# A two-layer encoder trunk: gates and branch projections with tokens as the stationary operand, seven task lanes, another order of the projections, one transform in plain fp32

## The chip, the cores and the metric

The kernel runs on one core of one Trainium2 chip, as one program. The metric is device time in microseconds (us). Before the change it is 1631.18 us, the median of three runs (1630.85 to 1631.53).

## The reference, cut to what matters

The trunk has two layers over 256 tokens of width 1024, all in float32. Each layer adds three sub-layers to x. The first one is where the change lies:

```python
h = rmsnorm(x, mix_norm_g)
proj = h @ w_in          # q, k, v, z, xbc, dt, f_in, gate_logit: 14400 columns
y_attn    = attention(q, k, v) @ w_b_attn      #  512 -> 1024, three groups merged
y_ssd     = ssd(xbc, dt, z)    @ w_b_ssd       # 2048 -> 1024
f = fft2(f_in (256 tokens, 6 groups, 256), axes=(tokens, channels), "ortho").real
y_fourier = f @ w_b_fourier                    # 1536 -> 1024
gates = sigmoid(gate_logit + gate_bias)        # (256, 3, 1024)
merged = gates[0] * y_attn + gates[1] * y_ssd + gates[2] * y_fourier
x = x + merged @ w_out
```

Then come cross-attention into 256 memory tokens and a SwiGLU feed-forward part of width 2816; the change does not touch these two.

## The kernel before, in words

**Split products.** Weights reach the chip as fp32. Each piece of weights (usually 128 x 2048 numbers, 1 MB) is split: ScalarE casts it to fp32r (`wh`, line 323), VectorE subtracts to get the rest (`wl`, line 324). Activations are kept as such a pair too. One product is then three fp32r matmuls on TensorE: high by high, high by low, low by high (`mm3`). Elsewhere (attention scores, the SSD products of lines 848 and 849, attention times values in line 648) a product is one plain fp32 matmul.

**Two forms of projection.** `lin` (lines 353 to 355) holds 128 tokens by 128 inputs as the stationary operand and streams 512 weight columns past it: the result has tokens on the partitions. `lina` (lines 414 to 416) holds 128 x 128 weights stationary and streams the 256 tokens: the result has output channels on the partitions. Before the change, the gate logits, the three branch projections and the x/B/C channels go through `lina`; q, k, v, z, the Fourier inputs, the output projection and cross-attention go through `lin`; the feed-forward part uses both.

**Pieces in order.** `stream_plan` writes out the order of the pieces from the list `ORDER`, and SyncE's DMA queue loads them in it. There are three buffers for raw pieces (`wr`) and three for split ones (`wh`, `wl`), so a split can start only when TensorE is done with the piece three before.

**Background tasks.** All that follows a projection (convolution, SSD, attention, Fourier, gating) is written as Python generators in queues called lanes ("n", "s", "a", "f"). Behind each piece, `pump` gives the lanes some us of credit, and `step` runs the next task's next stage, if the pools of 4 KB and 2 KB slots have room. A stage that says LATER waits for some pumps. When a slot is wanted and few are free, stages are run at once, whatever the credit. The tile framework then orders the instructions of each engine.

**Around the change.** `gates` (line 1013) applies tanh on ScalarE with the bias as a per-partition operand (line 1021). `branch` (line 1027) multiplies gate and projection into `mg` on VectorE (lines 1036 to 1039). `merge_fin` (line 1129) splits the merged channels as they are, since the output projection wants channels on the partitions. The Fourier inputs' even and odd token sums are split (lines 1088 to 1092), and `fourier_chunk` transforms positions with `mm3` on 128 x 128 tiles, in its first loop; the channel transform is a second `mm3`.

Of the kernel before, what the change touches and what calls it, by code (L numbers as in the profile page):

```python
# [34 lines left out]
LANES = ("n", "s", "a", "f")  # L35
# [10 lines left out]
ORDER = ("f0 f1 f2 bc k0 x0 G2 BF x1 q0 v0 q2 x2 q1 k1 v1 k2 v2 z1 x3 G0 z0 z2 z3 BA G1").split()  # L46


def stream_plan():
    plan = []  # L50

    def half(w, n0, h, k0=0):
        plan.append((w, k0 + 4 * h, 4, n0, 512))

    def full(w, n0):
        half(w, n0, 0)
        half(w, n0, 1)
# [9 lines left out]
    def blocks(w, kt, n):  # L67
        for n0 in range(0, 1024, n):
            plan.append((w, 0, kt, n0, n))

    for tok in ORDER:
        k, g = tok[0], int(tok[1]) if len(tok) > 1 and tok[1].isdigit() else 0
        if k == "f":
            full("w_in", F0 + 512 * g)
        elif k == "G":
            for c in range(4):
                wide("w_in", G0 + 1024 * g + 256 * c)
        elif tok == "BF":
            blocks("w_branch_fourier", 12, 128)
        elif tok == "BA":  # L80
            blocks("w_branch_attn", 4, 512)
# [24 lines left out]
    plan.append(("w_ffn_down", 20, 2, 0, 1024))  # L106
    return plan
# [5 lines left out]
POFF = [sum(PSIZE[:i]) for i in range(NPIECE + 1)]  # L113


def pack_weights(inputs):
    out = np.empty((L, POFF[-1]), np.float32)
# [54 lines left out]
def trunk(ctx: ExitStack, tc: tile.TileContext, a, out):  # L172
# [367 lines left out]
    def attn_group(l, g, qt, kt_, vt, gqk, R):  # L540
# [43 lines left out]
        O = R["O"]  # L584
        for tt in range(2):
# [23 lines left out]
            if tt or not g:  # L609
                free(bts[tt])  # L610
# [42 lines left out]
            else:  # L653
                for hh in range(4):
                    hs = slice(hh * P, hh * P + P)
                    o = O[:, tt, hs]
                    V.tensor_scalar(o, o, sc[:, 3, hh:hh + 1], None, op0=ALU.mult)
                    V.scalar_tensor_tensor(o, po[:, hs], sc[:, 0, hh:hh + 1], o, op0=ALU.mult, op1=ALU.add)
            yield 1.6
        free(qt, vt, kT)  # L660
        if g == 2:
            yield LATER
            yield 2, 0
            oT = R["oT"] = ftiles(1)
            for tt in range(2):
                pt = tp()
                for hh in range(4):
                    T.transpose(pt[:, hh * P:(hh + 1) * P], O[:, tt, hh * P:(hh + 1) * P], idn)
                put_f(pt, oT[0], tt, par=True)
                yield 0.7  # L670
            free(O)
            R["a"] = True
# [219 lines left out]
    def dft_parts(R):  # L892
        yield 3, 0
        r = s4([P, 6, P])
        nc.sync.dma_start(r, a["c_dft"])
        hi, lo = R["dft"] = s4([P, 6, P], F32R), s4([P, 6, P], F32R)
        A.copy(hi, r)
        V.tensor_sub(lo, r, hi.bitcast(F32))
        free(r)
        yield 0.9  # L900

    def fourier_chunk(l, c, f, FT, R):
# [5 lines left out]
        dh, dl = R["dft"]  # L908
# [23 lines left out]
        for cp_ in range(2):  # L932

            qc, qs = (t[:, :4 * n].rearrange("p (j k) -> p j k", j=4) for t, n in ((tp(), 66), (tp(), 64)))
            with ordered():
                for m, o, k0, k1 in ((2, qc, 0, 66), (4, qs, 64, 128)):
                    m += cp_
                    mm3(o, dh[:, m, :], dl[:, m, :], gp[0][:, cp_, :, k0:k1], gp[1][:, cp_, :, k0:k1], True, True)
# [50 lines left out]
    for l in range(L):  # L989
# [19 lines left out]
        gbc = sm([P, 24], "gbc", bufs=1)  # L1009
        nc.sync.dma_start(gbc, a["gateb"][l])  # L1010
        V.tensor_scalar(gbc, gbc, 0.5, None, op0=ALU.mult)
# [15 lines left out]
        def branch(act, np_, ga, fin=None):  # L1027
            first = not mg
            if first:
                mg.extend(s4([P, 4, S]) for _ in range(2))  # L1030

            def f(n0, ps):
                c, n = n0 // P, ps.shape[1]
                g_, m_ = (t[c // 4][:, c % 4:c % 4 + n, :] for t in (ga, mg))
# [5 lines left out]
                if fin:  # L1040
                    fin(c, n, m_)
            lina(act, np_, f)
# [24 lines left out]
        def xbc_pieces(blk, fin_of):  # L1067
            def f(n0, ps):
                pair = (n0 - X0) // 256 - blk // 2
                bg(conv_pair(ps, blk + 2 * pair, cw, fin_of(pair)))  # L1070
            lina(hb, 2, f)

        ys, FT, yT = {}, {}, {}
        bg(dft_parts(R), "f")
        for n, tok in enumerate(ORDER):
            k, g = tok[0], int(tok[1]) if tok[1].isdigit() else 0
            sg = [2] if n == 0 else None
            if k == "f":
                ft = (s4([P, 2, 512], F32R), s4([P, 2, 512], F32R))

                fs = []

                def f_done(tt, ch, ps, ft=ft, fs=fs):
                    if tt == 0:
                        fs.extend((s2([P, 512]), s2([P, 512])))
                        A.copy(fs[0], ps)
                        return
                    V.tensor_add(fs[1], fs[0], ps)
                    V.tensor_sub(fs[0], fs[0], ps)
# [7 lines left out]
            elif tok == "bc":  # L1097
# [4 lines left out]
                bg(cb_task(l, Bt, Ct, R))  # L1102
            elif k == "x":
                xT = s4([P, 2, 512])
                xbc_pieces(4 * g, lambda pr: x_fin([xT], pr))
                bg(ssd_group(l, g, xT, R, Dbc, ys))
# [4 lines left out]
            elif k == "z":  # L1111
                zt = s4([P, 2, 512])
                lin(hb, 2, lambda tt, ch, ps, zt=zt: A.activation(zt[:, tt, :], ps, AF.Silu))
                bg(ssd_gate(l, g, zt, ys, yT))
            elif k == "G":
                ga = gates(g)
            elif tok == "BF":
                drain_until(lambda: R.get("f") == 3, "f")
                branch(fl(FT), 8, ga)
                free(*FT.values(), ga)  # L1120
            elif tok == "BA":
                drain_until(lambda: "oT" in R and R.get("a"), "a")
                branch(fl(R["oT"]), 2, ga)
# [10 lines left out]
        branch(fl(yT), 8, ga, merge_fin)  # L1134
        free(*yT.values(), ga, mg)
# [21 lines left out]
        lin(fl(mT), 4, residual(gbx, hx), seg=[1, 3])  # L1157
# [271 lines left out]
```

## Time and profile before

| what | value |
|---|---|
| profiled execution, whole | 1631.55 us |
| its span | 1629.8 us |
| median of three runs | 1631.18 us |
| TensorE busy | 1611.2 us, 99% |
| VectorE busy | 1164.7 us, 71% |
| ScalarE busy | 974.2 us, 60% |
| 16 DMA engines, mean share of the weight queue | 54.0% |

How to read the rows further down. A row of a group of instructions gives line, engine, operation, output<-inputs by name, size of the stationary operand, shape of what streams through, count, then busy us in total and mean ns of one. A matmul's own duration includes the time in which the next one already runs, so what a stream of matmuls costs is read from the distance of their starts in the timeline. A timeline row is: start in us, duration in us, engine, line, operation, count; a chain row is: start, us until the next step, what. A row of waits is: who waited, for whom, us in total, times, longest. A row of windows is: stretch, its length, busy us of each engine with its count, the granted clock as a share of full speed, the DMA share, GB/s.

### The profile page before, as it was taken

Reading aid. Unit: us, or ns where it says so; the run is one execution under the profiler, and the core shown is the slowest. Engines: PE = TensorE matmul, PEld = TensorE weight load, DVE = VectorE, ACT = ScalarE, POOL = GpSimd, SP = SyncE. Lnnn points to the kernel's source line nnn. Section 1 sums busy time; section 2 is a strip of 40 time slices with the busy share of each in tenths; the row PEclk is TensorE's granted clock in tenths of the full one; section 3 lists DMA queues with packets and bytes.
Section 4 is the critical chain, followed back from the end, with each engine's and each line's share of the span. In section 5 each row is a group of like instructions: output and inputs, shape, how many; then the busy total and the mean of one; then the engine's idle time right before and its main releaser. Section 6 shows DMA issues by size and latency. Waiting matters only on the chain.

```text
span 1629.8 us, 25584 instructions
## 1 busy us (share of the span) xinstructions
PE 1611.2 (99%) x10354; PEld 1454.3 (89%) x10354; DVE 1164.7 (71%) x1803; ACT 974.2 (60%) x1639; POOL 45.9 (3%) x47
## 2 busy tenths in 40 slices
PE   7999999999999999999999999999999999999998
PEld 6899988898998888999879998888989988889997
DVE  6898878788966665555479988868888676665543
ACT  6566667778745665444355667677786357554441
POOL 0000000000100100000000000000000001000000
PEclk9999999999999999999999999999999999999999
DMA  8445754656556544555553567555455555445552
GB/s 280 152 153 188 237 202 149 203 172 178 194 177 228 178 156 156 206 181 192 181 170 123 175 213 226 195 170 180 168 187 194 182 206 181 143 158 179 183 189 93
DMA packets 84302, 296.52 MB, mean 182 GB/s; under 512 B 7529, under 2 KB 46825, under 8 KB 53976
## 3 DMA queue, kind: packets, MB, share of 16 engines
q1 hardware_dynamic: 84184, 294.89, 54.0%
q8 instruction: 81, 1.33, 0.3%
q14 instruction: 37, 0.30, 0.1%
HBM read 293.65 MB, written 1.22 MB: 181 GB/s over the span
## 4 chain that ended last, share of the span: by engine, by line
PE 94%; ACT 3%; DVE 2%; issue 1%; POOL 0%; DMA 0%; SPq 0%; DVEq 0%; ACTq 0%; POOLq 0%
PE acc L354 14%; PE acc L355 14%; PE acc L353 14%; PE acc L415 13%; PE acc L414 13%; PE acc L416 13%; PE tp L848 2%; ACT wh L323 2%; PE tp L353 1%; PE tp L355 1%; PE tp L354 1%; PE tp L849 1%; PE tp L473 1%; PE tp L648 1%; PE tp L603 1%; DVE wl L324 1%
## 5 line engine op out<-in xcount | busy, mean ns | idle before, releaser
L324 DVE TENSOR_TENSOR wl<-wr,wh 128x2048 fp32r<-128x2048 f32 (+2 forms) x260 | 573.3, 2207 | 283.9 <-ACT wh L323 283.3
L323 ACT CAST wh<-wr 128x2048 fp32r<-128x2048 f32 (+2 forms) x260 | 477.4, 1839 | 402.2 <-issue 181.2
L414 PE MATMUL acc<-s,wh 128*128 128x256 f32 x1856 | 527.9, 285 | 0.0
L415 PE MATMUL acc<-s,wh 128*128 128x256 f32 x1856 | 526.6, 284 | 0.0
L416 PE MATMUL acc<-s,wl 128*128 128x256 f32 x1856 | 525.5, 283 | 0.0
L353 PE MATMUL acc<-wh,s 128*128 128x512 f32 x1072 | 427.7, 399 | 0.0
L354 PE MATMUL acc<-wl,s 128*128 128x512 f32 x1072 | 424.4, 396 | 0.4 <-DVE wl L324 0.4
L355 PE MATMUL acc<-wh,s 128*128 128x512 f32 x1072 | 423.7, 396 | 0.0
L415 PEld LDWEIGHTS acc<-s,wh 128*128 128x128 f32 x1856 | 356.1, 192 | 1.3 <-issue 0.5
L414 PEld LDWEIGHTS acc<-s,wh 128*128 128x128 f32 x1856 | 355.8, 192 | 1.6 <-issue 0.9
L416 PEld LDWEIGHTS acc<-s,wl 128*128 128x128 f32 x1856 | 355.8, 192 | 0.0
L355 PEld LDWEIGHTS acc<-wh,s 128*128 128x128 f32 x1072 | 203.6, 190 | 41.6 <-issue 1.4
L353 PEld LDWEIGHTS acc<-wh,s 128*128 128x128 f32 x1072 | 203.9, 190 | 41.2 <-issue 1.9
L354 PEld LDWEIGHTS acc<-wl,s 128*128 128x128 f32 x1072 | 203.8, 190 | 41.0 <-issue 0.9
L689 DVE SCALAR_TENSOR_TENSOR s<-s,cw,s 128x253 f32<-128x253 f32 (+2 forms) x288 | 121.7, 476 | 1.1 <-ACT s L686 0.7
L820 ACT ACTIVATE s<-s,nacs 128x128 f32<-128x128 f32 x128 | 44.6, 394 | 15.2 <-DMA s<-dd 13.9
L823 ACT ACTIVATE s<-s,dt 128x128 f32<-128x128 f32 x128 | 43.8, 395 | 2.7 <-DVE s L604 2.1
L821 DVE SCALAR_TENSOR_TENSOR s<-s,nacs,s 128x128 f32<-128x128 f32 x128 | 41.5, 344 | 5.0 <-ACT s L820 5.0
L353 PE MATMUL tp<-s,s 128*128 128x256 f32 (+2 forms) x152 | 42.8, 284 | 1.7 <-ACT s L923 1.5
L355 PE MATMUL tp<-s,s 128*128 128x256 f32 (+2 forms) x152 | 42.6, 283 | 0.5 <-DVE s L1092 0.5
L354 PE MATMUL tp<-s,s 128*128 128x256 f32 (+2 forms) x152 | 42.4, 280 | 0.0
L489 DVE TENSOR_TENSOR s<-tp,s 128x512 fp32r<-128x512 f32 x56 | 36.6, 683 | 5.6 <-ACT s L488 5.6
(223 smaller groups left out, 1419.7 us busy)
## 6 DMA issues: line engine op xcount, KB each, us to landing
wr<-in_wstream SPq DMA_DIRECT2D x236, 1024.0 KB, 4.9
s<-dd SPq DMA_DIRECT2D x32, 512.0 KB, 5.3
wr<-in_wstream SPq DMA_DIRECT2D x16, 768.0 KB, 4.4
s<-vd SPq DMA_DIRECT2D x12, 256.0 KB, 6.1
wr<-in_wstream SPq DMA_DIRECT2D x8, 256.0 KB, 4.7
s<-in_ssd_norm_g SPq DMA_DIRECT2D x8, 256.0 KB, 5.4
s<-in_memT SPq DMA_DIRECT2D x4, 512.0 KB, 5.9
X<-in_x SPq DMA_DIRECT2D x2, 512.0 KB, 3.8
```

Source lines behind the costliest of these rows:

```text
L323: A.copy(hi[:, c], raw[:, c])
L324: V.tensor_sub(lo[:, c], raw[:, c], hi[:, c].bitcast(F32))
L353: T.matmul(o, sh, mh, start=start, stop=False)
L354: T.matmul(o, sh, ml, start=False, stop=False)
L355: T.matmul(o, sl, mh, start=False, stop=stop)
L414: T.matmul(o, hi[:, w0:w0 + P], sh[:, k, :], start=kt == 0, stop=False)
L415: T.matmul(o, hi[:, w0:w0 + P], sl[:, k, :], start=False, stop=False)
L416: T.matmul(o, lo[:, w0:w0 + P], sh[:, k, :], start=False, stop=kt == npk - 1)
L689: V.scalar_tensor_tensor(v[:, b, i0:i1], u[:, b, i0 + k - 3:i1 + k - 3], c[:, k:k + 1], v[:, b, i0:i1], op0=ALU.mult, op1=ALU.add)
L820: A.activation(E[:, j, :], b[:, 1, :], AF.Identity, bias=nacs[:, tt, 32 + hf:33 + hf])
L821: V.scalar_tensor_tensor(E[:, j, :], b[:, 0, :], nacs[:, tt, hf:hf + 1], E[:, j, :], op0=ALU.add, op1=ALU.min)
L823: A.activation(W[:, j, :], cbd[:, tt, 0, :], AF.Copy, scale=dt[:, tt, hf:hf + 1])
```

## The change

Seven edits. (1) `gates` goes through `lin`: its bias is a row of the weight stream, spread over the partitions by a DMA; VectorE adds it, then ScalarE's tanh. (2) `branch` goes through `lin`, and the three branch weights come as pieces of 4 x 128 inputs by 512 columns. (3) The merged result now has tokens on the partitions, so `merge_task` transposes it on TensorE before the split. (4) The Fourier inputs stay plain fp32, the position transform is one plain fp32 matmul where it was three fp32r ones, and only the channel matrices are split. (5) Seven lanes: convolutions and gating in "c", the two token tiles of an attention group as tasks of their own in "t0" and "t1"; `attn_out` is a task by itself. (6) The SSD group and the gating are queued when their inputs are written. (7) `ORDER` is changed.

```diff
-LANES = ("n", "s", "a", "f")
+LANES = ("n", "s", "c", "a", "t0", "t1", "f")
-ORDER = ("f0 f1 f2 bc k0 x0 G2 BF x1 q0 v0 q2 x2 q1 k1 v1 k2 v2 z1 x3 G0 z0 z2 z3 BA G1").split()
+ORDER = ("f0 f1 f2 bc x0 k0 G2 BF x1 q0 v0 x2 q1 k1 v1 x3 z0 q2 k2 v2 z1 G0 z2 z3 BA G1").split()
...
         elif k == "G":
-            for c in range(4):
-                wide("w_in", G0 + 1024 * g + 256 * c)
+            full("w_in", G0 + 1024 * g)
+            full("w_in", G0 + 1024 * g + 512)
         elif tok == "BF":
-            blocks("w_branch_fourier", 12, 128)
+            chunks("w_branch_fourier", 3)
...
-    blocks("w_branch_ssd", 16, 128)
+    chunks("w_branch_ssd", 4)
...
-        for tt in range(2):
+        def tile_task(tt):
+            O = R["O"]
             yield (0, 3) if g else (2, 1)
...
+        for tt in range(2):
+            bg(tile_task(tt), f"t{tt}")
...
-                        mm3(pg[:, ct, e * P:e * P + P], f[0][:, e, cs], f[1][:, e, cs], dh[:, e, :], dl[:, e, :],
-                            True, True)
+                        T.matmul(pg[:, ct, e * P:e * P + P], f[:, e, cs], dt_[:, e, :], start=True, stop=True)
...
         def gates(b):
-            ga = [s4([P, 4, S]) for _ in range(2)]
-
-            def f(n0, ps):
-                c = (n0 - G0) // P
-                for j in range(2):
-                    k = c + j - 8 * b
-                    A.activation(ga[k // 4][:, k % 4, :], ps[:, j, :], AF.Tanh, scale=0.5, bias=gbc[:, c + j:c + j + 1])
-            lina(hb, 4, f)
+            ga = [s4([P, D]) for _ in range(2)]
+            o = POFF[-1] + D * b
+            gbb = bcast(a["wstream"][l:l + 1, o:o + D], D)
+            c0 = (G0 + D * b) // 512
+
+            def f(tt, ch, ps):
+                cs = slice((ch - c0) * 512, (ch - c0) * 512 + 512)
+                g_ = ga[tt][:, cs]
+                V.tensor_add(g_, ps, gbb[:, cs])
+                A.activation(g_, g_, AF.Tanh, scale=0.5)
+            lin(hb, 4, f)
+            free(gbb)
             return ga
...
-        def branch(act, np_, ga, fin=None):
+        def branch(act, nh, ga, fin=None):
...
-            lina(act, np_, f)
+            lin(act, 2 * nh, f, nk=4 * nh)
...
-                    for e, t in enumerate(fs[::-1]):
-                        A.copy(ft[0][:, e, :], t)
-                        V.tensor_sub(ft[1][:, e, :], t, ft[0][:, e, :].bitcast(F32))
-                    free(fs)
...
-        def merge_fin(c, n, m_):
-            hi, lo = (t[:, c % 4:c % 4 + n, :] for t in mT[c // 4])
-            A.activation(hi, m_, AF.Copy, scale=0.5)
-            V.scalar_tensor_tensor(lo, m_, 0.5, hi.bitcast(F32), op0=ALU.mult, op1=ALU.subtract)
...
+        def merge_task(tt, ch, m_):
+            yield SOON
+            pt = tp()
+            for k in range(4):
+                T.transpose(pt[:, k * P:(k + 1) * P], m_[:, k * P:(k + 1) * P], idn)
+            put_f(pt, mT[ch], tt, scale=0.5)
+            merged.append((tt, ch))
+            yield 0.6
...
-        lin(fl(mT), 4, residual(gbx, hx), seg=[1, 3])
+        lin(fl(mT), 4, residual(gbx, hx), seg=[1, 3], before=all_merged)
```

**TensorE at the first position transform (layer 1, behind the second Fourier projection).** Before: `s_24`, `s_25` are the split inputs, `s_39`, `s_40` the split matrices, `tp` the transform's banks, `acc` the projection under way.

```order
L353 MATMUL tp_114<-s_39_300,s_24_219 128x128
L353 MATMUL tp_111<-s_39_300,s_24_219 128x128
L354 MATMUL acc_118<-wl_289,s_8_136 128x512
L355 MATMUL acc_118<-wh_288,s_9_137 128x512
L353 MATMUL acc_115<-wh_322,s_6_134 128x512
```

After: `s_23` is the plain input, `s_34` the plain matrix.

```order
L357 MATMUL acc_115<-wh_313,s_6_134 128x512
L358 MATMUL acc_115<-wl_314,s_6_134 128x512
L940 MATMUL tp_114<-s_34_292,s_23_216 128x128 x4
L940 MATMUL tp_111<-s_34_292,s_23_216 128x128 x4
L359 MATMUL acc_115<-wh_313,s_7_135 128x512
```

All eight products of a chunk now stand together, one instruction each; before they stood in threes, begun with the high parts and interleaved with the projection.

**TensorE at the end of the mixer of layer 1.** Before, the last SSD branch products (`acc_115`, 256 columns) are followed at once by the output projection (`wh_5297`).

```order
L414 MATMUL acc_115<-s_483_4919,wh_5236 128x256
L415 MATMUL acc_115<-s_484_4920,wh_5236 128x256
L416 MATMUL acc_115<-s_483_4919,wl_5237 128x256
L353 MATMUL acc_116<-wh_5297,s_485_4933 128x512
L354 MATMUL acc_116<-wl_5298,s_485_4933 128x512
```

After: `wh_4488` is the first piece of the output projection, with 24 products; `s_176` and `s_177` are the merged tiles of the two token halves.

```order
L357 MATMUL acc_117<-wh_4488,s_472_4300 128x512
L358 MATMUL acc_117<-wl_4489,s_472_4300 128x512
L359 MATMUL acc_117<-wh_4488,s_473_4301 128x512
L1174 MATMUL tp_113<-idn,s_176_1478 128x128 x4
L1174 MATMUL tp_114<-idn,s_177_1479 128x128 x4
L357 MATMUL acc_118<-wh_4524,s_472_4300 128x512
```

The last eight transposes of the merged result stand behind the 24 products of the output projection's first piece, and the next piece reads the first half of the inputs again (`s_472`).

**VectorE around the second gate's projection (G0) of layer 1.** `wl_3532` and `wl_3793` are the splits of two pieces that follow each other; line 673 and 674 scale and add an attention group's result, line 1042 adds the gate's bias. Before there was no row of this last kind, and the longest such stretch had 50 instructions between two splits (`wl_4259` and `wl_4331`).

```order
L328 TENSOR_TENSOR wl_3532<-wr_3314,wh_3531 128x2048
L493 TENSOR_TENSOR s_388_3539<-tp_111,s_387_3538 128x4x128
L493 TENSOR_TENSOR s_388_3539<-tp_114,s_387_3538 128x4x128
L872 TENSOR_TENSOR s_367_3348<-s_391_3565,tp_113 128x512
L620 SCALAR_TENSOR_TENSOR s_396_3576<-tp_112,ars_3370,s_371_3367 128x128
```

The stretch goes on for 69 more instructions and ends so:

```order
L673 TENSOR_SCALAR s_274_2450<-s_274_2450,asc_3648 128x128
L328 TENSOR_TENSOR wl_3793<-wr_3346,wh_3792 128x2048
L674 SCALAR_TENSOR_TENSOR s_274_2450<-tp_114,asc_3648,s_274_2450 128x128
L1042 TENSOR_TENSOR s_386_3537<-acc_116,s_412_3766 128x512
L1042 TENSOR_TENSOR s_401_3629<-acc_117,s_412_3766 128x512
```

More background work (74 instructions: 12 of 128x512, 39 of 128x128, 23 tiny ones) now stands between two splits than anywhere before.

## Rows read from the trace of the kernel before

**Rows 1.** The page: engines' busy time, and the granted clock by slices.

```profile
PE 1611.2 (99%) x10354; PEld 1454.3 (89%) x10354; DVE 1164.7 (71%) x1803; ACT 974.2 (60%) x1639; POOL 45.9 (3%) x47
...
PEclk9999999999999999999999999999999999999999
```

**Rows 2.** The page: the chain that ended last, by engine.

```profile
PE 94%; ACT 3%; DVE 2%; issue 1%; POOL 0%; DMA 0%; SPq 0%; DVEq 0%; ACTq 0%; POOLq 0%
```

**Rows 3.** All waits of TensorE, the whole span.

```profile
PE tp L521 <- ACT s L514: 7.9, 1, 7.9
PE tp L473 <- DVE s L465: 2.4, 5, 0.8
PE tp L353 <- ACT s L923: 1.5, 1, 1.5
...
PE tp L355 <- DVE s L1092: 0.5, 2, 0.3
```

**Rows 4.** Groups of TensorE instructions, shapes apart.

```profile
L414 PE MATMUL acc<-s,wh 128*128 128x256 f32 x1856 | 527.9, 285 | 0.0
...
L353 PE MATMUL acc<-wh,s 128*128 128x512 f32 x1072 | 427.7, 399 | 0.0
...
L648 PE MATMUL tp<-s,s 128*128 128x128 f32 x128 | 16.7, 276 | 0.0
```

**Rows 5.** Timeline of TensorE in a gate projection (`lina`), 26 starts apart.

```profile
119.86 0.28 PE L415 MATMUL acc<-s,wh 128*128 128x256 f32 x1
...
122.98 0.28 PE L414 MATMUL acc<-s,wh 128*128 128x256 f32 x1
```

**Rows 6.** Timeline of TensorE in the feed-forward output (`lin`), 13 starts apart.

```profile
767.05 0.39 PE L355 MATMUL acc<-wh,s 128*128 128x512 f32 x1
...
770.00 0.39 PE L353 MATMUL acc<-wh,s 128*128 128x512 f32 x1
```

**Rows 7.** Chain: plain fp32 records, `lin` with every second token stationary, transposes.

```profile
396.26 0.89 PE tp L648 x8
...
399.75 0.23 PE acc L353
...
401.61 0.23 PE acc L355
...
404.34 0.86 PE tp L849 x2
...
407.52 0.94 PE tp L848 x8
...
451.60 1.75 PE tp L886 x16
```

**Rows 8.** Timeline of TensorE in the position transform before.

```profile
50.16 0.27 PE L353 MATMUL tp<-s,s 128*128 128x128 f32 x1
...
50.38 0.28 PE L355 MATMUL tp<-s,s 128*128 128x128 f32 x1
```

**Rows 9.** Windows: three stretches of layer 1, all engines.

```profile
60.00:100.00 40.00, 39.90 (x296) 37.86 (x295) 39.37 (x84) 24.33 (x44) 0.00 (x0) 1.00 0.48 159
250.00:290.00 40.00, 40.00 (x210) 34.03 (x209) 28.88 (x46) 31.25 (x78) 0.00 (x0) 1.00 0.46 148
381.00:421.50 40.50, 40.44 (x243) 33.98 (x241) 37.47 (x100) 38.86 (x84) 0.00 (x0) 1.00 0.54 160
```

**Rows 10.** Group on VectorE: an add of 128x512 numbers from PSUM.

```profile
L1148 DVE TENSOR_TENSOR X<-X,acc 128x512 f32<-128x512 f32 x24 | 16.4, 683 | 26.2 <-PE acc L355 26.2
```

**Rows 11.** Timeline of VectorE: two tiny operations, eight of one kind, a split.

```profile
394.75 0.16 DVE L621 TENSOR_TENSOR asc<-asc 128x4 f32<-128x4 f32 x1
394.84 0.16 DVE L626 TENSOR_TENSOR rsum<-rsum,asc 128x4 f32<-128x4 f32 x1
...
404.51 2.19 DVE L824 SCALAR_TENSOR_TENSOR s<-s,dt,s 128x128 f32<-128x128 f32 x8
...
408.42 2.28 DVE L324 TENSOR_TENSOR wl<-wr,wh 128x2048 fp32r<-128x2048 f32 x1
```

More of the change, by code (lines that the diff above doesn't have):

```diff
@@ L65, in kmajor, with chunks @@
             half(w, 512, h)
-    def blocks(w, kt, n):
-        for n0 in range(0, 1024, n):
-            plan.append((w, 0, kt, n0, n))
+    def chunks(w, nh):
+        for n0 in (0, 512):
+            for h in range(nh):
+                half(w, n0, h)
     for tok in ORDER:
@@ L113 @@
 POFF = [sum(PSIZE[:i]) for i in range(NPIECE + 1)]
+NBIAS = 3 * D
 def pack_weights(inputs):
-    out = np.empty((L, POFF[-1]), np.float32)
+    out = np.empty((L, POFF[-1] + NBIAS), np.float32)
+    out[:, POFF[-1]:] = np.asarray(inputs["gate_bias"])
     for l in range(L):
@@ L583, in attn_group, with tile_done @@
             R["s"] = sm([P, 2, 4], "rsum", bufs=1)
-        O = R["O"]
-        for tt in range(2):
+        left = [0, 1]
+        def tile_done(tt):
+            left.remove(tt)
+            if left:
+                return
+            free(qt, vt, kT)
+            if g:
+                free(bts[0])
+            if g == 2:
+                bg(attn_out(R), "a")
+        def tile_task(tt):
+            O = R["O"]
             yield (0, 3) if g else (2, 1)
@@ L608, in attn_group @@
             free(qT)
-            if tt or not g:
+            if not g:
                 free(bts[tt])
@@ L658, in attn_group, with attn_out @@
                     V.scalar_tensor_tensor(o, po[:, hs], sc[:, 0, hh:hh + 1], o, op0=ALU.mult, op1=ALU.add)
+            tile_done(tt)
             yield 1.6
[L660 to L672, printed above, removed]
+        for tt in range(2):
+            bg(tile_task(tt), f"t{tt}")
+    def attn_out(R):
+        O = R["O"]
+        yield LATER
+        yield 2, 0
+        oT = R["oT"] = ftiles(1)
+        for tt in range(2):
+            pt = tp()
+            for hh in range(4):
+                T.transpose(pt[:, hh * P:(hh + 1) * P], O[:, tt, hh * P:(hh + 1) * P], idn)
+            put_f(pt, oT[0], tt, par=True)
+            yield 0.7
+        free(O)
+        R["a"] = True
     def conv_pair(ps, blk, cw, fin):
@@ L907, in fourier_chunk @@
         Gt = (s4([P, 2, 2, S], F32R), s4([P, 2, 2, S], F32R))
-        dh, dl = R["dft"]
+        dt_, hl = R["dft"]
         for j in range(2):
@@ L1008, in trunk, with f @@
         R = {}
[L1009 to L1011 removed]
         def gates(b):
[L1015 to L1022 removed]
+            ga = [s4([P, D]) for _ in range(2)]
[9 more added lines that the diff above has]
+            free(gbb)
             return ga
         mg = []
[L1027 removed]
+        def branch(act, nh, ga, fin=None):
             first = not mg
             if first:
[L1030 to L1034, printed above, removed]
+                mg.extend(s4([P, D]) for _ in range(2))
+            def f(tt, ch, ps):
+                cs = slice(ch * 512, ch * 512 + 512)
+                g_, m_ = ga[tt][:, cs], mg[tt][:, cs]
                 if first:
@@ L1069, in f, with after_conv, task, ssd_start @@
                 pair = (n0 - X0) // 256 - blk // 2
-                bg(conv_pair(ps, blk + 2 * pair, cw, fin_of(pair)))
+                bg(conv_pair(ps, blk + 2 * pair, cw, fin_of(pair)), "c")
             lina(hb, 2, f)
+        def after_conv(f):
+            def task():
+                f()
+                yield 0.0
+            bg(task(), "c")
+        zts = {}
+        def ssd_start(g, xT):
+            def task():
+                for c in ssd_group(l, g, xT, R, Dbc, ys):
+                    yield c
+                if g in zts:
+                    bg(ssd_gate(l, g, zts[g], ys, yT), "c")
+                zts[g] = None
+            bg(task())
         ys, FT, yT = {}, {}, {}
@@ L1118, in trunk @@
                 drain_until(lambda: R.get("f") == 3, "f")
-                branch(fl(FT), 8, ga)
+                branch(fl(FT), 3, ga)
                 free(*FT.values(), ga)
@@ L1122, in trunk @@
                 drain_until(lambda: "oT" in R and R.get("a"), "a")
-                branch(fl(R["oT"]), 2, ga)
+                branch(fl(R["oT"]), 1, ga)
                 free(R["oT"], ga)
@@ L1127, in trunk, with all_merged @@
         mT = ftiles(2)
-        def merge_fin(c, n, m_):
-            hi, lo = (t[:, c % 4:c % 4 + n, :] for t in mT[c // 4])
-            A.activation(hi, m_, AF.Copy, scale=0.5)
-            V.scalar_tensor_tensor(lo, m_, 0.5, hi.bitcast(F32), op0=ALU.mult, op1=ALU.subtract)
-        branch(fl(yT), 8, ga, merge_fin)
-        free(*yT.values(), ga, mg)
+        merged = []
+        def merge_task(tt, ch, m_):
+            yield SOON
+            pt = tp()
+            for k in range(4):
[3 more added lines that the diff above has]
+            yield 0.6
+        branch(fl(yT), 4, ga, lambda tt, ch, m_: bg(merge_task(tt, ch, m_)))
+        free(*yT.values(), ga)
+        def all_merged():
+            drain_until(lambda: len(merged) == 4, "s")
+            free(mg)
+        drain_until(lambda: len(merged) >= 2, "s")
         mh = ftiles(2)
```

46 lines of the change are left out of this document (25 added, 21 removed).

## The prediction

> **What bounds the kernel now.** I read the page first, its busy shares and the chain that ended last, then TensorE's waits, then the timeline, for the distance between starts. TensorE is busy 99% of the span, at full granted clock (2.4 GHz) in every slice [rows 1], and 94% of the chain is TensorE's [rows 2]. Its waits are few: 7.9 us until the first inputs are there, and behind that 2.4, 1.5, 0.5 us and smaller ones [rows 3]. So the time is the number of matmuls by the distance of their starts, and an edit counts by what it takes out of that stream or by a new wait that it puts into it. VectorE and ScalarE matter only where they come too late with a split; in three stretches of layer 1 VectorE is busy 39.4 of 40, 28.9 of 40 and 37.5 of 40.5 us, and TensorE is never idle by more than 0.1 us [rows 9].
>
> The duration of a matmul in the groups (285 ns with 256 columns, 399 with 512, [rows 4]) overlaps the next one; the distance of starts is the price. With 256 columns: 119.86 to 122.98 us, 26 distances, 0.120 us each [rows 5]. With 512: 767.05 to 770.00 us, 13 distances, 0.227 us each [rows 6]. Two of 256 columns cost 0.240, so one of 512 in their place saves 0.013 us.
>
> **The change part by part.**
>
> Gates and branches in `lin`. Per layer, `lina` had three gates of 4 pieces by 48 matmuls (576), the Fourier branch 12 x 8 x 3 (288), attention 4 x 8 x 3 (96), SSD 16 x 8 x 3 (384): 1344, over two layers 2688 of the three groups' 3 x 1856 [rows 4]. 1344 of 512 columns come instead. 1344 x 0.0131 = -17.6 us. The bounds: `lin` does not always run at 0.227. Where every second token is stationary (q, k, v) eight distances take 399.75 to 401.61 us, 0.2325 each [rows 7], and a pair would save 0.0075, -10.1 us in all. Gates and branches read adjacent tokens, as in rows 6, so I take -17.6.
>
> The Trainium skill, "TensorE: Matmul & The Clock Gate", section "Back-to-back issue gap", gives an isolated warm distance of N/2.4 + 2.5 ns, by which a pair of 256 would cost 218 ns against 216, and this part -3.4 us. The trace disagrees by its rows 5 and 6, with 120 and 227 ns, so a matmul costs here some 13 ns beyond its columns.
>
> Plain fp32 position transform. Per chunk it was 8 products of three matmuls, 3 chunks in 2 layers: 144. Two distances take 50.16 to 50.38 us, 0.11 each [rows 8]. The plain product of the same 128 x 128 shape is in line 648: attention has 4 heads by 2, 1 and 1 key tiles in 2 token tiles and 2 layers, 64 instructions, and the trace has 128 records [rows 4], two each; eight records take 0.89 us [rows 7], 0.111 each. 48 products become 96 records: (96 - 144) x 0.111 = -5.3 us. If the new line took a record more than line 648 shows, three, the edit would be worth 0.
>
> The Trainium skill, "FP8 and Floating Point Precision", section "TensorE Precision Notes", says that a true fp32 product takes four passes, which speaks against this edit: four of 0.111 against three would be +5.3 us. The trace shows two records, each as long as one fp32r record of that width; so by the row it is a gain.
>
> Transposes of the merged result: 4 tiles by 4, two layers, 32 more. Sixteen transposes take 1.75 us [rows 7], 0.109 each: +3.5 us. Their latency: behind the last branch product come two 128x512 operations on VectorE (0.68 us each by [rows 10]), four transposes (0.44), ScalarE's cast and VectorE's rest, some 3 us. The order puts 24 products of the output projection in front (24 x 0.227 = 5.4 us), which do not need them. So I take no wait; without the cover it is 3 us a layer.
>
> Work of the other engines. The bias add puts 24 adds of 128x512 on VectorE (24 x 0.68 = 16 us by [rows 10]); the splits of the Fourier sums (12 of about that size) and the splits of the merged result in halves go or change place. The instruction count of VectorE falls by 26 in the changed order, its busy sum stays about 1165 us. The tanh of the gates becomes 24 operations of 512 columns where it was 48 of 256. All this hides under TensorE as long as no stretch runs out of time. The gate bias rows (512 KB each, six) go through SyncE's queue ahead of weight pieces; each waits there for a free slot, and behind it wait the next loads. Three raw and three split pieces are the cover, some 16 us of `lin` work (72 x 0.227) for the split ones alone. I put it at 0, with the jam below as its price.
>
> The wait that goes: TensorE waits 1.5 us for ScalarE (line 923) and 0.5 us for VectorE (line 1092) in the first Fourier chunks [rows 3], behind splits of sums that no longer exist. I take -1.5; the bounds are -2 and 0, since the first channel transform could wait as before.
>
> The new wait. With seven lanes and pools nearly empty at G0, stages are run in a lump there. From split `wl_3343` to split `wl_3793` the changed order has on VectorE 4 splits, 19 operations of 128x512, 66 of 128x128 and 29 tiny ones. These cost 2.28 us (a split), 0.68 (an add of that size, [rows 10]), 0.27 (2.19 for eight) and 0.09 (the distance of two tiny ones' starts, [rows 11]): 9.1 + 12.9 + 17.8 + 2.6 = 42.4 us. TensorE has, from the end of the piece three before the first of these splits, 123 products of 512 columns (27.9 us), 52 transposes (5.7), 24 plain products of 128 columns (5.3), 16 plain ones of 64 (32 records at 0.94 / 8 us: 3.8) and two of 512 (two records in 0.86 us each: 1.7, [rows 7]): 44.4 us. VectorE must be busy 95% of it. Before, in the tightest stretch, it was 92.5% (37.47 of 40.50), with TensorE idle 0.06 us [rows 9]. At that share it needs 42.4 / 0.925 = 45.8 us, 1.4 more than TensorE has. So I take 1.5 us a layer, +3 us, both layers being alike. At the 98% of the first stretch in rows 9 it would be 0; if VectorE reached only the 72% of the second stretch, it would need 58.9 us, 14.5 a layer, +29 us: these are the ends, and the nearest row is the 92.5%, the one stretch of the three in which splits are so far apart.
>
> Lanes and order of projections as such move the same matmuls about, and cost nothing where TensorE does not wait.
>
> The sum: -17.6 - 5.3 + 3.5 - 1.5 + 3.0 = -17.9 us. 1631.55 (the profiled execution, its span of 1629.8 and 1.75 around it) becomes 1613.65; the median before is 0.4 below the profiled execution, so I predict 1613.3 us.
>
> **The rivals.**
>
> A, the jam decides (slower side). VectorE's lump around G0, with its chain of ScalarE, POOL and transposes, keeps the split of the next piece back. For: 74 instructions between two splits, where the longest such stretch had 50. Against: 98% busy without a TensorE wait in 60 to 100 us [rows 9]. From a wait of 10.5 us a layer on all of the gain (20.9 us without the jam) is gone; at 14.5 a layer the time is 1631.2 - 20.9 + 29 = 1639. A half-grown jam of 6 a layer gives 1622.
>
> B, `lin` does not come at 0.227 in the new places, because the stream of stationary loads of a branch, or its banks, hold it at the 0.2325 of q, k, v or worse: 7.5 us less gain, 1621. With no gain per pair (0.240) it is 1631. The Trainium skill's rule above, 2.5 ns beyond the columns, would give 1627.5; rows 5 and 6 speak against it.
>
> C, the plain product takes four records: 192 for 144, +5.3 us where I have -5.3, so 1624. Against it stand the 128 records of line 648. It is what the Trainium skill's four passes would give, were each a record.
>
> D, more waits go than I count: those of 2.4 us behind the norms shrink too [rows 3], no jam comes, and the short stalls at tasks' ends go: 1607, 6 us less.
>
> **How the numbers follow.** Forecast (1608 to 1619) 0.68; A in its mild form 0.10, in its full form 0.04; B at 1621 0.05, with no gain 0.02; C 0.03; D 0.08. The range of 1606 to 1626 takes in mild A, B at 1621, C and most of D, and leaves out some 0.1. A run of this kernel tells 0.2%, 3.3 us, from no change. Slower by more than that needs the full A: 0.03. Within it: full A near its break-even or B without any gain, 0.03. Faster: the rest, 0.94.
>
> **What would show it.** TensorE's records fall from 10354 to about 8990 (1344 less in the projections, 48 less in the transform, 32 more). In the gates and branches starts should stand 0.227 us apart; were it 0.233 or more, B holds. The line of the plain transform should have 96 records of 0.11 us between starts. Around G0 of each layer, TensorE's wait for the split `wl` tells of A: up to 3 us a layer fits, 6 and more does not. At the output projection no wait for the merged tiles should stand. If the span falls but TensorE's waits other than the first grow above 15 us, the sum was right by accident.

## The result, and the profile after

The changed kernel takes 1613.95 us (median; three of its four runs, 1612.18 to 1614.32, are compared, the fourth ran at a mean granted clock of 0.852 and took 1738.66), the kernel before 1631.36 beside it: a ratio of 0.9888 [0.9869, 0.9908]. Forecast were 1613.3, between 1606 and 1626. The profiled execution is 1612.18 us, its span 1610.1 us.

From the page of the changed kernel: busy time, share of the span and instructions of each engine, the granted clock in 40 slices, and the chain's shares by engine (of before: [rows 1, 2]):

```profile
PE 1592.1 (99%) x8994; PEld 1381.0 (86%) x8994; DVE 1163.8 (72%) x1777; ACT 956.5 (59%) x1587; POOL 43.8 (3%) x47
...
PEclk9999999999999999999999999999999999999999
...
PE 91%; DVE 4%; ACT 2%; DMA 1%; POOL 1%; issue 1%; SPq 0%; DVEq 0%; ACTq 0%; POOLq 0%
```

TensorE is as full as before, with 1360 records less: 10354 became 8994, and 1344 + 48 - 32 is 1360. Its busy time falls by 19.1 us, from 1611.2 to 1592.1; its idle time (span less busy time) is 18.0 us, and was 18.6. Its waits (us in total, times, longest; of before: [rows 3]):

```profile
PE tp L525 <- ACT s L518: 7.8, 1, 7.8
PE tp L477 <- DVE s L469: 2.3, 6, 0.5
PE acc L358 <- DVE wl L328: 1.6, 2, 0.8
PE tp L907 <- DVE s L674: 1.4, 2, 0.7
PE tp L1241 <- DVE s L1236: 0.6, 4, 0.2
```

The two waits of the first Fourier chunks (1.5 and 0.5 us) are gone. The wait for a split `wl` (line 358) is 1.6 us, where the view of before lists one of 0.4; new are 1.4 us of a line-907 transpose behind VectorE's last work on an attention group (line 674). All waits that the view lists come to 13.7 us, and to 13.8 before.

Groups of the changed kernel by form (count | busy us, mean ns | idle before):

```profile
L418 PE MATMUL acc<-s,wh 128*128 128x256 f32 x960 | 273.3, 285 | 0.0
...
L940 PE MATMUL tp<-s,s 128*128 128x128 f32 x96 | 12.8, 278 | 0.0
...
L1174 PE MATMUL tp<-idn,s 128*128 128x128 f32 x32 | 4.5, 272 | 0.0
```

Of 1856 matmuls of 256 columns a line [rows 4], 960 are left. The plain transform has 96 records for 48 products, so two each, and the merged result has its 32 transposes. Eight transform records in the chain of the changed kernel (start, us until the next step):

```profile
49.72 0.89 PE tp L940 x8
```

The first and the last of 14 neighbours in its first gate projection (timeline):

```profile
117.72 0.39 PE L358 MATMUL acc<-wl,s 128*128 128x512 f32 x1
...
120.66 0.39 PE L359 MATMUL acc<-wh,s 128*128 128x512 f32 x1
```

0.89 / 8 is 0.111 us a record; 2.94 / 13 is 0.226 us a matmul, where [rows 6] give 0.227.

### The profile page after: what moved, and what is told of

It is laid out like the page before. It is cut to its first block, busy times and chain, and to the rows that moved or that the text cites. A ratio compares the mean times of both kernels' runs of the same rounds, so it can differ in the third digit from the quotient of the medians.

```text
span 1610.1 us, 22777 instructions
## 1 busy us (share of the span) xinstructions
PE 1592.1 (99%) x8994; PEld 1381.0 (86%) x8994; DVE 1163.8 (72%) x1777; ACT 956.5 (59%) x1587; POOL 43.8 (3%) x47
## 4 chain that ended last, share of the span: by engine, by line
PE 91%; DVE 4%; ACT 2%; DMA 1%; POOL 1%; issue 1%; SPq 0%; DVEq 0%; ACTq 0%; POOLq 0%
PE acc L358 20%; PE acc L357 20%; PE acc L359 20%; PE acc L418 7%; PE acc L419 7%; PE acc L420 7%; PE tp L869 1%; PE tp L477 1%; PE tp L357 1%; PE tp L359 1%; PE tp L358 1%; PE tp L619 1%; DVE wl L328 1%; PE tp L940 1%; ACT wh L327 1%; PE tp L870 1%
## 5 line engine op out<-in xcount | busy, mean ns | idle before, releaser
L328 DVE TENSOR_TENSOR wl<-wr,wh 128x2048 fp32r<-128x2048 f32 (+1 forms) x256 | 572.6, 2239 | 278.5 <-ACT wh L327 277.9
L327 ACT CAST wh<-wr 128x2048 fp32r<-128x2048 f32 (+1 forms) x256 | 477.6, 1867 | 387.8 <-PE acc L359 184.3
L357 PE MATMUL acc<-wh,s 128*128 128x512 f32 x1520 | 604.4, 398 | 0.1
L358 PE MATMUL acc<-wl,s 128*128 128x512 f32 x1520 | 599.6, 395 | 1.6 <-DVE wl L328 1.6
L359 PE MATMUL acc<-wh,s 128*128 128x512 f32 x1520 | 596.2, 393 | 0.0
L357 PEld LDWEIGHTS acc<-wh,s 128*128 128x128 f32 x1520 | 287.9, 189 | 59.3 <-issue 1.4
L359 PEld LDWEIGHTS acc<-wh,s 128*128 128x128 f32 x1520 | 287.8, 189 | 58.0 <-issue 0.4
L418 PE MATMUL acc<-s,wh 128*128 128x256 f32 x960 | 273.3, 285 | 0.0
L419 PE MATMUL acc<-s,wh 128*128 128x256 f32 x960 | 271.7, 283 | 0.0
L420 PE MATMUL acc<-s,wl 128*128 128x256 f32 x960 | 271.6, 283 | 0.0
L418 PEld LDWEIGHTS acc<-s,wh 128*128 128x128 f32 x960 | 184.1, 192 | 1.1 <-issue 0.7
L419 PEld LDWEIGHTS acc<-s,wh 128*128 128x128 f32 x960 | 184.2, 192 | 0.8 <-issue 0.5
L420 PEld LDWEIGHTS acc<-s,wl 128*128 128x128 f32 x960 | 184.1, 192 | 0.0
L710 DVE SCALAR_TENSOR_TENSOR s<-s,cw,s 128x254 f32<-128x254 f32 (+2 forms) x288 | 120.9, 476 | 0.3
L841 ACT ACTIVATE s<-s,nacs 128x128 f32<-128x128 f32 x128 | 46.4, 392 | 13.4 <-DVE s L852 5.6
```

Source lines behind the costliest of these rows:

```text
L327: A.copy(hi[:, c], raw[:, c])
L328: V.tensor_sub(lo[:, c], raw[:, c], hi[:, c].bitcast(F32))
L357: T.matmul(o, sh, mh, start=start, stop=False)
L358: T.matmul(o, sh, ml, start=False, stop=False)
L359: T.matmul(o, sl, mh, start=False, stop=stop)
L418: T.matmul(o, hi[:, w0:w0 + P], sh[:, k, :], start=kt == 0, stop=False)
```

## The experiments

Medians, with the ratio to the kernel before in the same set of runs; "a gain of" is against that kernel. Edits are named by their numbers (1) to (7) of the section on the change; "..." in a code cut stands for lines left out. Busy and idle time are TensorE's, from the page of the profiled execution: idle is the span less the busy time.

**One part at a time.** First the plain transform alone, edit (4):

```diff
...
-    mm3(pg[:, ct, e * P:e * P + P], f[0][:, e, cs], f[1][:, e, cs], dh[:, e, :], dl[:, e, :],
-        True, True)
+    T.matmul(pg[:, ct, e * P:e * P + P], f[:, e, cs], dt_[:, e, :], start=True, stop=True)
...
```

> The kernel before with the plain fp32 position transform alone (inputs kept plain, only the channel matrices split). My theory: 96 records of 0.111 us in place of 144, and the 1.5 us wait in the first Fourier chunk goes: about 7 us less than before, 1624.5. Rival, four records for a plain product: 5 us more than before, 1636. Rival, the transform hides beside the projections: no change.

Measured: 1622.13, 0.9939 [0.9927, 0.9952], a gain of 10 us. The span falls by 9.2 (1629.8 to 1620.6): the busy time falls by 6.7 of it (1611.2 to 1604.5), where 48 records of 0.111 make 5.3, and the listed waits by 2.2 (13.8 to 11.6).

Then gates, branches and merged result, edits (1) to (3), with the old lanes and the old order:

```diff
-    lina(hb, 4, f)
+    lin(hb, 4, f)
...
-    lina(act, np_, f)
+    lin(act, 2 * nh, f, nk=4 * nh)
```

> The kernel before with gates and branches through lin (512 weight columns streaming past stationary tokens) and the transposes of the merged result, old lanes and old order of projections. My theory: -17.6 + 3.5 = -14 us, about 1617. Rival, a pair of 256 columns costs hardly more than one of 512: -3.4 + 3.5, no change at 1631. Rival, the distance is that of q, k, v (0.2325 us): -6.6 us, 1625.

Measured: 1656.42, 1.0153 [1.0139, 1.0167], slower by 24 us where a gain of 14 was expected.

Then lanes, tasks and order, edits (5) to (7), without the others:

```diff
-LANES = ("n", "s", "a", "f")
+LANES = ("n", "s", "c", "a", "t0", "t1", "f")
```

> The kernel before with the seven lanes, the tasks of their own and the new order of projections alone. My theory: the same matmuls move about, and the lump around G0 costs 0 to 3 us a layer: 1631 to 1637. Rival, the lanes were what brought the gain, by taking waits out of TensorE: 10 us or more off, 1621 or less.

Measured: 1641.34, 1.0054 [1.0041, 1.0068], slower by 9 us, more than any of the expectations. Its span is 8.1 us longer than before; TensorE's waits in it:

```profile
PE tp L521 <- ACT s L514: 8.0, 1, 8.0
PE acc L354 <- DVE wl L324: 2.8, 3, 1.4
PE tp L473 <- DVE s L465: 2.4, 5, 0.7
PE tp L603 <- ACT s L792: 2.0, 2, 1.2
PE tp L353 <- ACT s L940: 1.5, 1, 1.5
PE tp L903 <- DVE s L670: 1.4, 2, 0.7
```

With the smaller rows behind them they sum to 20.4 us, 6.6 more than before: the new ones are for `wl` and for small tasks (lines 603 and 903). So most of the loss is waits. By the page, 6.1 of the 8.1 us are idle time and 2.0 are busy time (1613.2 against 1611.2) with the same matmuls; where those 2.0 arise is not shown.

**The changed kernel without its schedule.** Edits (1) to (4), with the old lanes, tasks and order:

```diff
-LANES = ("n", "s", "c", "a", "t0", "t1", "f")
+LANES = ("n", "s", "a", "f")
...
-ORDER = ("f0 f1 f2 bc x0 k0 G2 BF x1 q0 v0 x2 q1 k1 v1 x3 z0 q2 k2 v2 z1 G0 z2 z3 BA G1").split()
+ORDER = ("f0 f1 f2 bc k0 x0 G2 BF x1 q0 v0 q2 x2 q1 k1 v1 k2 v2 z1 x3 G0 z0 z2 z3 BA G1").split()
...
```

> The changed kernel with the old four lanes, old tasks and old order of projections (both of the matmul edits stay). My theory: without the lump the time is at or a little below the changed kernel, 1610 to 1614, the sum of the two edits alone. Rival, with gates and branches in lin the old schedule jams and the lanes are needed: over 1617.

Measured: 1644.45, 1.0076 [1.0063, 1.0089], slower than before by 12 us: the theory missed by 30 us, and the rival held. Its waits of TensorE:

```profile
PE tp L525 <- ACT s L518: 9.6, 1, 9.6
PE tp L672 <- DVE s L662: 5.6, 4, 2.6
PE tp L642 <- ACT s L620: 4.1, 2, 2.1
PE tp L652 <- ACT s L643: 4.1, 2, 2.1
PE tp L595 <- DVE s L493: 3.8, 2, 1.9
PE acc L359 <- DVE s L493: 3.0, 2, 1.5
```

Lines 595 to 672 are attention. The waits of lines 642, 652 and 672 stand in front of the attention branch; the timeline of layer 1 there (start, us, [idle before]):

```profile
407.24 1.48 PE L642 MATMUL tp<-idn,s 128*128 128x128 f32 x4 [2.06 <-ACT s L620]
410.85 2.08 PE L652 MATMUL tp<-s,s 128*128 128x128 f32 x8 [2.13 <-ACT s L643]
415.53 0.73 PE L672 MATMUL tp<-idn,s 128*128 128x128 f32 x2 [2.60 <-DVE s L662]
```

And five stretches of 4 us (stretch, length, busy us of PE, PEld, DVE, ACT, POOL, granted clock, DMA share, GB/s):

```profile
400.00:404.00 4.00, 4.00 (x20) 3.29 (x19) 4.00 (x5) 3.97 (x12) 0.00 (x0) 1.00 0.50 136
404.00:408.00 4.00, 1.84 (x10) 1.05 (x8) 3.13 (x14) 3.76 (x11) 0.69 (x1) 1.00 1.01 420
408.00:412.00 4.00, 1.81 (x7) 1.43 (x8) 2.97 (x5) 3.10 (x7) 0.00 (x0) 0.80 0.18 67
412.00:416.00 4.00, 1.40 (x7) 0.99 (x5) 3.22 (x16) 3.04 (x10) 0.00 (x0) 0.50 0.60 211
416.00:420.00 4.00, 3.83 (x10) 2.11 (x9) 4.00 (x12) 1.57 (x3) 0.00 (x0) 0.50 0.13 51
```

TensorE does one short thing, waits some 2 us for a softmax or a split, and goes on: a chain of small steps with nothing beside it. Behind two such waits the granted clock is 0.50 (1.2 GHz), also in the last stretch, where TensorE is busy 3.83 of 4.00 us. Not every wait does this: behind a single one of 1.89 us (line 595, until 379.55 us) the clock of layer 1 is at 0.50 from 380 to 383 us, and behind the same wait of layer 2 (until 1192.51 us) it stays at 1.00. In the order of issue, six stages of attention tasks stand directly ahead of the attention branch here: the branch needs their result, so they run at once, whatever the credit. In the kernel before and in the changed one none stands there. The program's own count of credit tells how far the background is behind: at G0 of layer 1 it stands at -7.2 us here and at +4.5 in the kernel before, and attention has one task more in its lane at its branch. The level at G0 alone does not tell, since in the changed kernel it is -5.2 with attention done in time. What tells is the work paid for by the attention branch: 175.9 us of it here, 190.5 in the kernel before and 196.9 in the changed one. The credit handed out until there is the same in all three (197.2 us, 3.4 for a piece of 1 MB), but what would lift the count above its cap of 6 us lapses: 22.5 us here, 11.9 before, 6.6 in the changed kernel. Up to the Fourier branch, here and before lie 0.2 us apart in this, and directly behind it 4.0, so the setback begins in edit (2). Why more credit lapses there was not taken apart, and that the lapsed credit is what makes the attention branch wait is argued from the count; the next run is its only test.

**Only the credit.** The last kernel again, with

```diff
-BUDGET = 3.4
+BUDGET = 3.8
```

> The kernel of e4 (both matmul edits, old four lanes, old order) with the pieces' credit for background stages raised from 3.4 to 3.8 us. In e4 TensorE waits around 400 to 420 us of layer 1 on attention stages run one by one in front of the attention branch, since the third attention group is not finished when that branch comes; with 3.8 it is finished. My theory now: that unfinished chain, not the load of VectorE, is what made e2 and e4 slow; so the jam goes and the time falls to the sum of the matmul terms, 1609 to 1614. Rival: gates and branches in lin leave VectorE and ScalarE too little time everywhere: it stays over 1630. Rival: in between, over 1617, if only the seven lanes can cover it.

Measured: 1611.29, 0.9874 [0.9859, 0.9888], 33.2 us below the same kernel with 3.4. Its waits of TensorE:

```profile
PE tp L525 <- DMA wr<-in_wstream: 10.1, 1, 10.1
PE tp L477 <- DVE s L469: 2.0, 5, 0.5
PE tp L890 <- DVE s L881: 0.9, 2, 0.6
PE tp L642 <- ACT s L620: 0.9, 2, 0.6
```

And two stretches of 20 us around the same place:

```profile
380.00:400.00 20.00, 19.74 (x112) 16.12 (x112) 18.54 (x68) 19.85 (x47) 0.70 (x1) 1.00 0.49 165
400.00:420.00 20.00, 20.00 (x98) 16.45 (x97) 19.00 (x33) 17.59 (x32) 0.00 (x0) 1.00 0.48 162
```

And the first row of both pages, with the credit of 3.4 and of 3.8:

```profile
PE 1604.5 (98%) x8994; PEld 1386.7 (84%) x8994; DVE 1166.6 (71%) x1777; ACT 958.0 (58%) x1587; POOL 43.0 (3%) x47
PE 1591.1 (99%) x8994; PEld 1380.6 (86%) x8994; DVE 1165.6 (72%) x1777; ACT 961.0 (60%) x1591; POOL 42.7 (3%) x47
```

Of the attention waits 0.9 us are left (line 642), and the clock stays at full speed there. Between the two spans lie 32.4 us (1642.5 and 1610.1): 19.0 of idle time, of which the listed waits make 18.3 (32.8 to 14.5), and 13.4 of busy time with the same 8994 records. The clock is part of the 13.4. A mean of 0.992 instead of 1.000 over 1642.5 us would be 13.1, but that counts waiting at the low clock too, and such waits are in the 19.0 already: from 412 to 416 us TensorE is busy 1.40 of 4.00. Counted for its busy time alone, in steps of 1 us, the low clock cost an estimated 9.5 us. The other 4 are not attributed.

**Credit for the projections alone.** Edits (1) to (3) with the credit of 3.8:

> The kernel before with gates, branches and the transposes of the merged result (as e2), and credit 3.8, so that attention is finished at its branch. My theory: now the term stands alone, -17.6 + 3.5 = -14 us: 1617.6, with the transform's term (e1: -10) to come on top in e5. Rival, the spacing of q, k, v: -6.6, 1625. Rival, the page's small price for each matmul as the Trainium skill, TensorE: Matmul & The Clock Gate, section Back-to-back issue gap, gives it: no change, 1631.

Measured: 1621.31, 0.9932 [0.9919, 0.9944], a gain of 11 us, where the same edits with 3.4 lost 24. It and the transform alone (10) add up to the run with both (20.4). From its page:

```profile
PE 1598.7 (99%) x9042; PEld 1385.1 (85%) x9042; DVE 1172.3 (72%) x1789; ACT 967.6 (60%) x1603; POOL 42.7 (3%) x47
```

The busy time falls by 12.5 us; the span, 1620.8, only by 9.0, since the idle time grows by 3.5, and 2.0 of that are the first wait (9.9 us, 7.9 before). The kernel before was not run with the credit of 3.8, so a gain by the credit alone is not excluded; its listed waits behind the first come to 5.9 us.

**The old transform in the changed kernel.** Edits (1) to (3) and (5) to (7):

> The changed kernel with the position transform as before (three fp32r products, inputs split). My theory: 7 to 10 us more than the changed kernel, as e1 showed the transform to be worth alone: 1621 to 1624. Rival, the new lanes had already taken the wait that the transform took (1.5 us) and the stalls behind it: 5 us more, 1619.

Measured: 1627.91, 0.9975 [0.9965, 0.9985]; the transform is worth 14 us in the changed kernel. Its waits have rows that the changed kernel's have not, the two largest:

```profile
PE tp L795 <- DVE s L715: 1.2, 2, 1.1
PE tp L357 <- ACT s L816: 1.2, 2, 0.9
```

The spans are 15.5 us apart (1625.6 and 1610.1): 5.3 for the records, 5.4 for the waits (19.1 and 13.7), and some 1.6 for the clock, 0.96 in the one stretch from 40 to 80 us. The other 3 are not attributed; they lie in the busy time, which is 10.0 longer (1602.1 and 1592.1).

**The order of projections.** The changed kernel with the old `ORDER`:

> The changed kernel with the old order of projections, new lanes and tasks kept. Attention is finished when its branch comes here too, and the lump of stages around G0 is smaller. My theory: 1609 to 1615, like the changed kernel or a little below. Rival, the new order is the part that is needed with lin: over 1620.

Measured: 1613.83, 0.9889 [0.9875, 0.9904]. The order of projections, edit (7), is worth nothing. Lanes and tasks, edits (5) and (6), were not taken apart from each other.

**The price of a matmul, asked in the changed kernel.** Gates and branches in `lin`, each matmul of 512 columns cut in two of 256 (but for the first and the last of a group), 1248 matmuls more:

```diff
...
+    for n3, (st_, mv) in enumerate(((sh, mh), (sh, ml), (sl, mh))):
+        a0, z0 = k == 0 and n3 == 0, k == nk - 1 and n3 == 2
+        step_ = 512 if a0 or z0 else cols
+        for q0 in range(0, cw, step_):
+            qs_ = slice(q0, q0 + step_)
+            T.matmul(o[:, qs_], st_[:, kt % 4, ts_], mv[:, qs_], start=a0, stop=z0)
...
-    lin(hb, 4, f)
+    lin(hb, 4, f, cols=256)
...
-    lin(act, 2 * nh, f, nk=4 * nh)
+    lin(act, 2 * nh, f, nk=4 * nh, cols=256)
```

> The changed kernel with the 512-column matmuls of gates and branches cut in two of 256 columns (but for the first and the last of each group): same stationary tokens, same columns, 1248 matmuls more. My theory, a fixed price for each matmul beyond its columns: starts 0.120 us apart and +1248 x 0.0131 = +16.4 us, 1630. Rival, the price came from streaming tokens past stationary weights, whatever the width: no change, 1614.

Measured: 1627.06, 0.997 [0.9958, 0.9983], 13.1 us above the changed kernel, 0.0105 us a matmul. That is below the 0.0131 of the two spacings, but the intervals of the two ratios hold both. From its page:

```profile
PE 1607.1 (99%) x10242; PEld 1446.6 (89%) x10242; DVE 1164.2 (72%) x1777; ACT 956.5 (59%) x1587; POOL 43.5 (3%) x47
```

The busy time is 15.0 us above the changed kernel's, 0.0120 a matmul, and the idle time 1.5 below it (span 1623.6): the waits for `wl`, 1.6 us in the changed kernel, are not listed here. Four and then two halves, from its timeline:

```profile
117.80 0.64 PE L400 MATMUL acc<-wh,s 128*128 128x256 f32 x4
118.28 0.40 PE L400 MATMUL acc<-wl,s 128*128 128x256 f32 x2
118.52 0.40 PE L400 MATMUL acc<-wh,s 128*128 128x256 f32 x2
```

0.48 us for four, 0.24 for two: 0.120 each, as in [rows 5].

Then the gates with every second token stationary, as q, k and v have it (the gates' tokens then stand in another order than the branches', which this kernel leaves so: only the time is asked):

```diff
-    lin(hb, 4, f)
+    lin(hb, 4, f, par=True)
```

> The changed kernel with the gates computed on every second token in each half (tokens at a distance of two as the stationary operand, as q, k, v have it); the gates' tokens then stand in another order than the branches', which the text leaves as it is: only the time is asked. 576 matmuls of 512 columns are concerned. My theory: the distance of starts goes from 0.227 to 0.2325 us there: +3.2 us, 1617. Rival, the 0.2325 belongs to what runs beside q, k, v and not to the distance of the tokens: no change, 1614.

Measured: 1616.57, 0.9905 [0.9891, 0.9918], 2.6 us above the changed kernel, with overlapping intervals; the busy time is 3.0 longer (1595.1 and 1592.1), near the 3.2 expected. The first and last of 14 neighbours in its gate projection, 3.03 / 13 = 0.233 us each:

```profile
118.80 0.39 PE L358 MATMUL acc<-wl,s 128*128 128x512 f32 x1
...
121.83 0.39 PE L359 MATMUL acc<-wh,s 128*128 128x512 f32 x1
```

So the slower spacing of [rows 7] belongs to the stride of the stationary operand, not to q, k and v.

**Further on the same way.** In the changed kernel the feed-forward gate and up projections go through `lin` too, all but their last 256 columns:

```diff
-    full("w_ffn_gate", 0)
-    full("w_ffn_up", 0)
-    for c in range(512, DFF, 256):
-        wide("w_ffn_gate", c)
-        wide("w_ffn_up", c)
+    for c in range(0, 2560, 512):
+        full("w_ffn_gate", c)
+        full("w_ffn_up", c)
+    wide("w_ffn_gate", 2560)
+    wide("w_ffn_up", 2560)
...
```

> The changed kernel with the feed-forward gate and up projections through lin as well, but for the last 256 columns: 1536 matmuls of 256 columns become 768 of 512, and 64 transposes are added. My theory: -768 x 0.0131 = -10.1 and +64 x 0.109 = +7.0, so -3.1 us against the changed kernel, 1611. Rival, the transposes wait on VectorE and ScalarE: 1616 or more. Rival, the distance of starts saves nothing: +7, 1621.

Measured: 1611.26, 0.9873 [0.9859, 0.9888], 2.7 us below the changed kernel with overlapping intervals; the busy time falls by 2.9 (1592.1 to 1589.2), about what the columns price (3.1 expected).

The same edit on the kernel with the old schedule and the credit of 3.8:

> The kernel of e5 (both matmul edits, old lanes and order, credit 3.8) with the feed-forward projections of e7. My theory: the two gains are on separate stages and add up: 1611.3 - 2.8 = 1608.5, 3 us below either and 23 below the kernel before. Rival, the credit also drives the feed-forward stages and the transposes come at a worse place: 1611 or more.

Measured: 1608.58, 0.9855 [0.9842, 0.9869], with 8290 TensorE records, the fastest of all. It has no seven lanes and no new order.

## Why the prediction was right, point by point

- **Gates and branches, -17.6, and transposes, +3.5.** Together -14.1 forecast; alone (run with the credit of 3.8) TensorE's busy time falls by 12.5 us, and the median by 11. The spacing is as read: 0.226 in the gates, 0.120 for two halves. The size was a little high: by the halves a pair saves 0.0120 us and not 0.0131, and 1344 of it, 16.1, less 3.5 for the transposes is 12.6. Rival B fails where it was named: adjacent tokens do not fall to 0.2325, every second token does. The Trainium skill's isolated distance ("TensorE: Matmul & The Clock Gate", "Back-to-back issue gap") would have made the halves cost 1248 times 2.5 ns, an estimate of 3.1 us; 13.1 were measured.
- **The plain transform, -5.3, and its wait, -1.5.** The term was too small, the mechanism right: two records of 0.111, but a gain of 10 us alone and 14 in the changed kernel. Alone the busy time falls by 6.7 where 5.3 were forecast, and the listed waits by 2.2 where 1.5 were; in the changed kernel 5.4 us of waits are at stake. So a transform with no split inputs takes more waits out around it than the one that was named. Rival C fails by the 96 records. The Trainium skill's four passes ("FP8 and Floating Point Precision", "TensorE Precision Notes") stand as two records of the length of one fp32r record each; no run shows what happens inside one.
- **The jam around G0, +3.0.** Two waits, 1.6 for `wl` and 1.4 behind line 674, make 3.0 us, 0.8 and 0.7 in each layer. The place is as forecast, but the wait that was named, for the split, is only half of the size; that the other one fills it up is luck. From VectorE's timeline of the changed kernel in layer 1, two splits with none between them:

```profile
357.93 2.28 DVE L328 TENSOR_TENSOR wl<-wr,wh 128x2048 fp32r<-128x2048 f32 x1
...
380.38 2.28 DVE L328 TENSOR_TENSOR wl<-wr,wh 128x2048 fp32r<-128x2048 f32 x1
```

What waits for the second of them, in TensorE's timeline, [idle before]:

```profile
382.71 0.50 PE L358 MATMUL acc<-wl,s 128*128 128x512 f32 x1 [0.80 <-DVE wl L328]
```

And the stretch around them in the view of windows:

```profile
340.00:400.00 60.00, 58.36 (x314) 48.04 (x313) 53.62 (x134) 48.29 (x102) 4.33 (x3) 1.00 0.50 175
```

  The splits start 22 us apart, and TensorE waits 0.80 us for the second. VectorE is busy 53.62 of 60 us, 89% (91% from 337.0 to 382.7 us, the stretch of the term), near the 92.5% on which the term was put. Rival A in full fails here.
- **No wait at the output projection.** None is listed. The 24 products in front cover the transposes.
- **"Lanes and order of projections as such move the same matmuls about, and cost nothing where TensorE does not wait."** This step failed. It is true of the order (1613.83 and 1613.95), not of lanes and tasks. Alone they cost 9 us. Beside edits (1) to (3) it is about 7 (1627.91 and 1621.31) and with all edits 2.7 (1613.95 and 1611.29), but there the run without the lanes has the credit of 3.8, so these two hold the credit's part too. The condition in the sentence is the point: TensorE does wait, since small tasks put their short chains elsewhere. And the step missed the other side: with the old schedule and the same credit the forecast gain would have been a loss of 12 us. The lanes prevent that, and 0.4 us more credit does it a little better: 1611.29 against 1613.83 for lanes and tasks with the old order, no run of the one within the range of the other.
- **The number.** The matmul terms come to -19.4 us (-17.6 - 5.3 + 3.5), and TensorE's busy time fell by 19.1: that is the mechanism of the forecast, and it held, the projections giving 1.6 less and the transform 1.4 more. The waits were put at +1.5, and the idle time fell by 0.6: in the runs with one part each, the transform takes waits out (2.2 us) and lanes and tasks put them in (6.6). That the median lies only 0.65 us from the forecast is luck, since the three runs are 2.1 us apart and these errors offset. "If the waits other than the first grow above 15 us, the sum was right by accident" did not happen (5.9 us), so the test that the prediction named would not have found the lanes' part.

A wait ahead of a stage as the way to a slower kernel (rival A's kind) is real, but at the attention branch, where tasks are left over, and not at G0 for lack of VectorE.

Open: why more credit lapses from the Fourier branch on; what the credit of 3.8 does to the kernel before and to the changed kernel, neither of which was run; TensorE's first wait lies between 7.7 and 10.1 us in the profiled executions, which nothing here explains; 3 us of the transform's worth in the changed kernel; 2 us of the lanes' cost alone; 4 us of the loss with attention left over.

## What to carry to other kernels

Where one engine is 99% busy, count its instructions and price them by the distance of their starts; that part of a forecast holds. When an edit changes the form or number of pieces, look also at where the background work then stands: a task left over at the point where its result is needed runs as a chain of small steps, and the clock can fall on top of it. Before a schedule is rewritten, try the one number that sets its pace.

## What the runs showed of the hardware

A 512-column matmul whose stationary operand takes every second element costs 0.233 us instead of 0.226. A plain fp32 product of 128 x 128 x 128 costs two records of 0.111 us, less than the three of a split product. And the clock can make waits dearer than they look: in the run with attention left over, the listed waits cost 18.3 us, and TensorE's work at the low clock an estimated 9.5 more, since behind two waits of 2 us the granted clock stood at 0.50 from 412 to 420 us, at work or not. A wait of 1.89 us brought it down in one layer and not in the other.
